# Three of twelve modulation vectors: rows of weights added up on VectorE, one burst of products with ones

## The chip, the cores and the metric

The kernel runs on one core of a Trainium2 chip. The metric is the device time of one execution in microseconds (us). Engines are named as in the profile: PE is TensorE, DVE is VectorE, ACT is ScalarE, POOL is GpSimd, SP is SyncE, which issues nearly all transfers here. Each engine takes its instructions in one fixed order and waits at an instruction until what it needs is there.

## The reference, cut to what matters

Two layers of a diffusion backbone over 384 tokens (128 of a prompt, 256 of a sample). Each layer begins with six modulation vectors of 1024 numbers for each of two conditions:

```
mod = silu(cond) @ w_mod[l] + b_mod[l]          # (1024) @ (1024, 6144)
sh1, sc1, g1, sh2, sc2, g2 = split(mod, 6)      # vectors v = 0 .. 5
h = rms_norm(x, norm1) * (1 + sc1) + sh1
x = x + g1 * token_mixers(h)                    # attention, latent attention, Hyena convolution
h = rms_norm(x, norm2) * (1 + sc2) + sh2
x = x + g2 * conv_ffn(h)
```

So a layer needs vectors 0 and 1 at its first norm, vector 2 at the output projection, 3 and 4 at the second norm, and 5 at the end of the feed-forward part. Twelve vectors in all, written (layer, v) below: (0,0) to (1,5).

## The kernel before

All tokens stand side by side as 384 columns; a product with a 128x128 block of weights is three matmuls of 384 columns (`mm3`, L269 to L271), since weights and activations are split into a high and a low part. A weight load (`load_w`, L249) brings 1 MB into one of two buffers of `raw_ring`; ACT copies the high part (L231), DVE subtracts the low one (L235).

A modulation vector is made by `mod_vec`: four loads of 1 MB (L329, into `raw_ring`, or ahead of time into free slabs by the class `Ahead`), and for each load a burst of four matmuls with 32 weight columns and 512 moving columns (L343), which lie in four column groups of PE and so run side by side. Here the condition is the stationary operand and the weights of the model are the moving one. ACT then copies the sums out of PSUM, PE turns them by four transposes (L302) and DVE adds the bias (L238).

The work is written as Python generators that yield after each step. `weave` advances a main line and, at a rate (steps per step of the main line), side lines: `md` for the modulation vectors, `fl` for the filters of the Hyena part, `att` for attention. The framework's scheduler then puts the instructions of each engine in one order, by the order in which they were written, their priorities, and when it expects operands to be ready. Layer 0 makes vectors 2 to 5 beside its mixers; vectors (1,0) to (1,3) are loaded ahead and made around the norms, where PE has little else; (1,4) follows in layer 1's mixers, (1,5) at its second norm.

A norm (`norm_h`) is a chain over PE, ACT and DVE: sums of squares, square root, `ident` scaled (L391), a product (L394) that spreads the result over partitions; then for each of eight blocks a product on DVE, the modulation on ACT (L402), and a split into high (L409 on DVE, or L231 on ACT) and low (L238 or L235 on DVE) parts `h`. All products of the next stage wait for these blocks.

Names in the rows: `base` holds what lives long (`cT`, the condition; `mods`; `raw_ring`), `split` the split weights, `h` the split activations, `s` the slabs for everything short-lived, `extra` a slab of 3584 columns that attention uses too, `banks` PSUM.

## Time and profile before

| | before |
|---|---|
| median of 3 runs | 1494.21 us (1493.5 to 1496.85) |
| profiled execution | 1491.25 us, span 1489.4 us |
| PE busy | 1443.1 us, 97% of the span |
| DVE busy | 1004.1 us, 67% |
| ACT busy | 752.4 us, 51% |
| matmuls of `mod_vec` | twelve vectors of 4 bursts, 4 matmuls each |

The time of the profiled execution is 1.85 us more than its span, and 2.96 us less than the median. Matmuls are pipelined: the busy time of one overlaps the next, so the cost of a matmul in a stream is the distance from its start to the next start.

### The profile page before, as it was taken

The page shows a single profiled execution, that of the slowest core. Times are in us where ns is not written, and L with a number is a line of the kernel's source. Part 1 is how long each engine was busy: PE and PEld are TensorE (multiplying, and loading weights), DVE is VectorE, ACT ScalarE, POOL GpSimd, SP SyncE. Part 2 cuts the span into 40 slices and gives each one's busy share as a digit, 9 for nine tenths or more (in the row PEclk, how much of TensorE's full clock was granted, in tenths as well). Part 3 has the DMA queues.
Part 4 walks back from the last instruction along what each step waited for, and adds up shares of the span by engine and source line. Part 5 has one row for each costly group of instructions (what it writes and reads, how often), then busy time and mean ns, then how long its engine had stood idle before and what let it go on. Part 6 is the DMA issues. An engine that isn't in the chain of part 4 may idle for free.

```text
span 1489.4 us, 22058 instructions
## 1 busy us (share of the span) xinstructions
PE 1443.1 (97%) x8542; PEld 1334.6 (90%) x8542; DVE 1004.1 (67%) x1920; ACT 752.4 (51%) x1376; POOL 106.1 (7%) x133
## 2 busy tenths in 40 slices
PE   5799999999999999999998999999999999999997
PEld 2598899989888899999996988999998989999997
DVE  6868578547456886686766667874655677566674
ACT  4644366555544663453545444855555465344443
POOL 1223210000000001010000213000000000000000
PEclk9899999999999999999999999999999999999999
DMA  9444454343476533343276445233342534333431
GB/s 364 153 153 141 150 180 142 92 114 114 142 262 223 184 114 113 114 131 114 92 247 207 134 137 185 90 108 98 86 141 87 197 100 134 120 114 123 146 123 48
DMA packets 177497, 212.84 MB, mean 143 GB/s; under 512 B 24177, under 2 KB 160113, under 8 KB 177393
## 3 DMA queue, kind: packets, MB, share of 16 engines
q1 hardware_dynamic: 176528, 206.99, 42.9%
q0 software_dynamic: 864, 4.46, 0.9%
q8 instruction: 67, 1.10, 0.3%
q14 instruction: 38, 0.30, 0.1%
HBM read 209.29 MB, written 2.13 MB: 142 GB/s over the span
## 4 chain that ended last, share of the span: by engine, by line
PE 91%; DVE 5%; ACT 2%; DMA 1%; issue 1%; SPq 0%; DVEq 0%; ACTq 0%
PE banks L269 26%; PE banks L270 26%; PE banks L271 26%; PE banks L302 4%; PE banks L928 3%; PE banks L343 2%; DVE s L238 2%; PE banks L960 2%; DVE split L235 1%; DMA base<-in_w_in_dram 1%; PE banks L564 1%; DVE s L241 1%; ACT split L231 0%; PE banks L509 0%; ACT s L231 0%
## 5 line engine op out<-in xcount | busy, mean ns | idle before, releaser
L231 ACT ACTIVATE split<-base 128x1024 fp32r<-128x1024 f32 (+2 forms) x272 | 280.8, 1040 | 357.4 <-PE banks L270 245.4
L235 DVE TENSOR_TENSOR split<-base,split 128x1024 fp32r<-128x1024 f32 (+2 forms) x272 | 330.4, 1220 | 169.6 <-ACT split L231 169.2
L269 PE MATMUL banks<-h,split 128*128 128x384 f32 x1280 | 432.9, 342 | 6.6 <-DVE h L409 3.6
L270 PE MATMUL banks<-h,split 128*128 128x384 f32 x1280 | 434.3, 340 | 0.0
L271 PE MATMUL banks<-h,split 128*128 128x384 f32 x1280 | 432.6, 338 | 0.5 <-DVE split L235 0.5
L269 PEld LDWEIGHTS banks<-h,split 128*128 128x128 f32 x1280 | 240.9, 189 | 19.0 <-issue 7.9
L270 PEld LDWEIGHTS banks<-h,split 128*128 128x128 f32 x1280 | 241.4, 189 | 4.0 <-DVE h L409 0.8
L271 PEld LDWEIGHTS banks<-h,split 128*128 128x128 f32 x1280 | 241.1, 188 | 2.8 <-DVE split L235 0.8
L271 PE MATMUL banks<-s,split 128*128 128x384 f32 x672 | 225.4, 338 | 0.0
L270 PE MATMUL banks<-s,split 128*128 128x384 f32 x672 | 225.2, 337 | 0.0
L269 PE MATMUL banks<-s,split 128*128 128x384 f32 x672 | 223.5, 339 | 0.8 <-ACT s L231 0.5
L241 DVE SCALAR_TENSOR_TENSOR s<-banks,base,s 128x127 f32<-128x127 f32 (+1 forms) x448 | 172.3, 410 | 11.0 <-ACT s L423 7.1
L231 ACT ACTIVATE s<-banks 128x384 f32<-128x384 f32 (+11 forms) x212 | 94.5, 471 | 94.7 <-PE banks L302 39.6
L231 ACT ACTIVATE s<-s 128x512 fp32r<-128x512 f32 (+3 forms) x142 | 78.9, 561 | 106.3 <-DVE s L238 56.2
L269 PEld LDWEIGHTS banks<-s,split 128*128 128x128 f32 x672 | 125.7, 188 | 4.0 <-ACT s L231 1.0
L271 PEld LDWEIGHTS banks<-s,split 128*128 128x128 f32 x672 | 126.1, 188 | 1.7 <-DVE base L241 0.8
L270 PEld LDWEIGHTS banks<-s,split 128*128 128x128 f32 x672 | 126.1, 188 | 1.3 <-issue 0.2
L238 DVE TENSOR_TENSOR s<-banks,s 128x512 f32<-128x512 f32 (+3 forms) x132 | 81.7, 644 | 37.0 <-PE banks L271 19.4
L241 DVE SCALAR_TENSOR_TENSOR base<-banks,base 128x128 f32<-128x128 f32 (+1 forms) x128 | 46.9, 412 | 73.3 <-PE banks L271 73.3
L238 DVE TENSOR_TENSOR s<-s 128x256 f32<-128x256 f32 (+4 forms) x122 | 68.8, 576 | 27.4 <-ACT s L1231 8.8
L423 ACT ACTIVATE s<-banks,base 128x384 f32<-128x384 f32 x112 | 73.4, 655 | 14.8 <-PE banks L271 14.8
L302 PE MATMUL banks<-base,s 128*128 128x128 f32 x442 | 75.0, 274 | 1.0 <-DVE s L241 0.4
(146 smaller groups left out, 1719.9 us busy)
## 6 DMA issues: line engine op xcount, KB each, us to landing
base<-in_w_in_dram SPq DMA_DIRECT2D x40, 1024.0 KB, 5.5
base<-in_ffn_up_dram SPq DMA_DIRECT2D x40, 1024.0 KB, 5.2
base<-in_w_mod_dram SPq DMA_DIRECT2D x28, 1024.0 KB, 5.4
s<-in_w_mod_dram SPq DMA_DIRECT2D x14, 1024.0 KB, 7.8
base<-in_ffn_down_dram SPq DMA_DIRECT2D x16, 896.0 KB, 4.6
base<-in_w_branch_dram SPq DMA_DIRECT2D x24, 512.0 KB, 3.6
base<-in_w_out_dram SPq DMA_DIRECT2D x8, 1024.0 KB, 5.5
base<-in_ffn_down_dram SPq DMA_DIRECT2D x8, 1024.0 KB, 5.0
```

The source lines that it names most:

```text
L231: act.activation(out=out, in_=in_, func=AF.Copy, scale=scale)
L235: dve.tensor_tensor(out=lo, in0=src, in1=f(hi), op=ALU.subtract)
L238: dve.tensor_tensor(out=out, in0=a, in1=b, op=op)
L241: dve.scalar_tensor_tensor(out=out, in0=a, scalar=s, in1=b, op0=op0, op1=op1)
L269: pe.matmul(out, l[0], r[0], start=start, stop=False)
L270: pe.matmul(out, l[0], r[1], start=False, stop=False)
L271: pe.matmul(out, l[1], r[0], start=False, stop=stop)
L302: pe.transpose(out, in_, ident[:n, :n])
L343: last = pe.matmul(gv[32 * j:32 * j + 32], cT[:, 2 * k + j // 2], raw[:, j // 2, (j % 2) * 512:(j % 2) * 512 + 512], start=k == 0, stop=k ...
L423: act.activation(out=dst, in_=src, func=AF.Identity, scale=vec(l, w1), bias=vec(l, bias))
L928: pe.matmul(out, q_of(h)[:, i * 128:(i + 1) * 128], k, start=m == 0, stop=m == len(ks) - 1)
L960: last = pe.matmul(p[b:b + 64, u], v, pT, start=start, stop=stop, tile_position=(0, b)).ins
```

## The change

The vectors (0,3), (0,5) and (1,4) are made by a new generator `mod_wide`. It loads the weights in 16 pieces of 128 rows by 512 columns (256 KB each) into a ring of three buffers in `extra`. For each piece DVE multiplies the piece by the condition's value for that row and adds it to a sum, once for each of the two conditions (`stt`, 28 instructions of 128x512 for a vector; the first piece of each half is scaled by ACT, 4 instructions). The four sums (two halves, two conditions) are then added over the partitions by four matmuls with 32 columns of ones, in the four column groups. The copy, the four transposes and the bias stay.

The side line of layer 0 is now (0,3), (0,2), (0,4), at rate 0.8 through the Hyena part; (0,5) is woven into the output projection; (1,4) follows the steps woven into layer 0's feed-forward part.

```diff
+R_MW = 0.8
-    XA = Arena([Slab(ctx, tc, N_EXTRA, "extra"), *FA.slabs])
+    extra = Slab(ctx, tc, N_EXTRA, "extra")
+    XO, XA = Arena([extra]), Arena([extra, *FA.slabs])
...
+    def mod_wide(l, v):
+        ring, acc_b = Ring(XO, 3, 512), XO.alloc(2, 2, 512)
+        acc = acc_b.ap()
+        for hf in range(2):
+            col = v * 1024 + hf * 512
+            for k in range(KD):
+                raw = ring.get().ap()
+                sp.dma_start(out=raw, in_=w_mod[l, k * 128:(k + 1) * 128, col:col + 512])
+                for s in range(2):
+                    c, a = cT[:, k, s:s + 1], acc[:, hf, s]
+                    if k:
+                        stt(a, raw, c, a, ALU.mult, ALU.add)
+                    else:
+                        act.activation(out=a, in_=raw, func=AF.Copy, scale=c)
+                yield
+        ring.free()
+        for _ in range(2):
+            yield
+        gv = ps_of("md", 512)
+        last = None
+        for j in range(4):
+            with ExitStack() as order:
+                if last is not None:
+                    order.enter_context(tc.high_priority(offset=U_AV))
+                    order.enter_context(tc.issue_after(last))
+                last = pe.matmul(
+                    gv[32 * j:32 * j + 32], ones[:, 0:32], acc[:, j // 2, j % 2], start=True, stop=True,
+                    tile_position=(0, 32 * j),
+                ).ins
+        acc_b.free()
...
-        md = chain(*[mod_vec(l, v) for v in (2, 3, 4, 5)]) if l == 0 else chain(nxt.pop().steps, mod_vec(l, 4))
+        md = chain(mod_wide(l, 3), mod_vec(l, 2), mod_vec(l, 4)) if l == 0 else nxt.pop().steps
         banks(**PS_HY0)
-        weave(main, (md, R_MD), (fl, R_FL))
+        weave(main, (md, R_MW if l == 0 else R_MD), (fl, R_FL))
...
         finish(md)
+        md = mod_wide(l, 5) if l == 0 else iter(())
...
-        weave(out_proj(l, merged), (ah.loads, R_AH))
+        weave(out_proj(l, merged), (md, R_MW), (ah.loads, R_AH))
+        finish(md)
...
-            weave(main, (fl, R_FL2), (rest, R_RE))
+            weave(main, (fl, R_FL2), (chain(rest, mod_wide(l + 1, 4)), R_RE))
```

Where the instructions come to stand decides much, so three places are shown. Behind the change line numbers are larger by 2 (L238 becomes L240, L241 becomes L243, L269 to L271 become L271 to L273, L302 becomes L304, L343 becomes L345) or by 51 (L388 becomes L439, L409 becomes L460, L564 becomes L615).

First place, the first norm of layer 0. DVE before, from the scale of the norm (the 128x16 instruction of L241) to the first split blocks of `h`:

```order
L241 SCALAR_TENSOR_TENSOR base_101<-base_101 128x16
L238 TENSOR_TENSOR s_1_212<-s_1_147 128x256
L547 RECIPROCAL s_1_147<-s_1_147 128x4
L238 TENSOR_TENSOR s_1_212<-s_1_141 128x256
L409 CAST h_363<-s_1_107 128x384
L238 TENSOR_TENSOR s_1_107<-base_101,banks 128x384
L238 TENSOR_TENSOR h_363<-s_1_107,h_363 128x384
L238 TENSOR_TENSOR s_1_107<-base_101,banks 128x384
```

DVE behind the change, the end of the same stretch (`extra` is the new sum):

```order
L243 SCALAR_TENSOR_TENSOR extra_470<-extra_470,base_101 128x512
L598 RECIPROCAL s_1_147<-s_1_147 128x4
L460 CAST h_363<-s_1_107 128x384
L240 TENSOR_TENSOR s_1_107<-base_101,banks 128x384
L243 SCALAR_TENSOR_TENSOR extra_470<-extra_470,base_101 128x512
L240 TENSOR_TENSOR s_1_107<-base_101,banks 128x384
L460 CAST h_363<-s_1_107 128x384
L240 TENSOR_TENSOR s_1_107<-base_101,banks 128x384 x2
L237 TENSOR_TENSOR h_363<-s_1_107,h_363 128x384 x2
L243 SCALAR_TENSOR_TENSOR extra_470<-extra_470,base_101 128x512
L240 TENSOR_TENSOR h_363<-s_1_107,h_363 128x384
```

The first low part of `h` (the last row) stood two instructions behind the first CAST and stands ten behind it now; nine of the 28 new instructions for (0,3) lie ahead of it, all 28 between the last filter work ahead of the norm and the first outputs of the Hyena products. PE behind the change, where the products with ones of (0,3) come:

```order
L273 MATMUL banks<-h_363,split_362 128x384
L397 MATMUL banks<-extra_470,base_101 32x512 x2
L615 MATMUL banks<-s_1_141 128x256
L615 MATMUL banks<-s_1_212,s_1_141 128x256
L615 MATMUL banks<-s_1_141 128x256
L615 MATMUL banks<-s_1_212,s_1_141 128x256
L304 MATMUL banks<-base_101,s_1_107 128x128
L397 MATMUL banks<-extra_470,base_101 32x512
L603 MATMUL banks<-s_1_141,base_101 128x512
L304 MATMUL banks<-base_101,s_1_107 128x128
L397 MATMUL banks<-extra_470,base_101 32x512
L304 MATMUL banks<-base_101,s_1_107 128x128
```

The four matmuls are no one burst: they stand as two, one and one, with filter products and transposes between. Those of (0,5) stand as two and two, those of (1,4) together.

Second place, the end of layer 0's latent attention on DVE. Before, from the scaling of one softmax (L906) to the split of the outputs (L235 on `banks`):

```order
L904 RECIPROCAL s_5_3170<-s_5_3170 128x1
L906 TENSOR_SCALAR s_5_3170<-s_5_3170 128x384
L235 TENSOR_TENSOR split_362<-base_101,split_362 128x1024
L904 RECIPROCAL s_1_138<-s_1_138 128x1
L906 TENSOR_SCALAR s_1_138<-s_1_138,s_5_3170 128x384
L235 TENSOR_TENSOR split_362<-base_101,split_362 128x1024
L235 TENSOR_TENSOR s_1_135<-banks,s_2_2238 128x2x256
```

Behind the change, from the last softmax's maximum (L948) to the same split:

```order
L948 TENSOR_REDUCE s_5_3192<-banks 128x1
L243 SCALAR_TENSOR_TENSOR extra_470<-extra_470,base_101 128x512
L949 TENSOR_SCALAR s_5_3192<-s_5_3192 128x1
L240 TENSOR_TENSOR base_101<-banks,base_101 128x8 x2
L243 SCALAR_TENSOR_TENSOR extra_470<-extra_470,base_101 128x512 x2
L955 RECIPROCAL s_5_3192<-s_5_3192 128x1
L243 SCALAR_TENSOR_TENSOR extra_470<-extra_470,base_101 128x512
L957 TENSOR_SCALAR s_1_138<-s_1_138,s_5_3192 128x384
L243 SCALAR_TENSOR_TENSOR extra_470<-extra_470,base_101 128x512 x6
L237 TENSOR_TENSOR s_1_135<-banks,s_2_2265 128x2x256
```

The scheduler has pulled (0,5) and the beginning of (1,4) far ahead of where they are written: 38 of the new instructions lie in the last softmaxes of layer 0, four of them inside the last one's chain. The other 18 of (1,4) follow within the last branch and the output projection.

Third place, PE at the second norm of layer 0. Before (L269 is the feed-forward part's first product, L466 a filter product):

```order
L343 MATMUL banks<-s_1_111,base_101 32x512 x4
L343 MATMUL banks<-s_3_3224,base_101 32x512 x4
L343 MATMUL banks<-s_3_3558,base_101 32x512 x4
L343 MATMUL banks<-s_1_138,base_101 32x512 x4
L388 MATMUL banks<-base_101,s_5_3170 128x1 x3
L302 MATMUL banks<-base_101 128x128 x4
L466 MATMUL banks<-s_2_3622 64x384
L394 MATMUL banks<-s_2_3622,base_101 128x384
L343 MATMUL banks<-s_2_3622,base_101 32x512 x4
L343 MATMUL banks<-s_3_2566,base_101 32x512 x4
L343 MATMUL banks<-base_101 32x512 x8
L269 MATMUL banks<-h_363,split_362 128x384 x4
```

Behind the change:

```order
L304 MATMUL banks<-base_101 128x128 x4
L345 MATMUL banks<-s_2_3651,base_101 32x512 x4
L345 MATMUL banks<-s_3_2597,base_101 32x512 x4
L345 MATMUL banks<-base_101 32x512 x4
L439 MATMUL banks<-base_101,s_5_3192 128x1 x3
L517 MATMUL banks<-s_2_3651 64x384
L345 MATMUL banks<-base_101 32x512 x4
L445 MATMUL banks<-s_2_3651,base_101 128x384
L304 MATMUL banks<-base_101 128x128 x4
L271 MATMUL banks<-h_363,split_362 128x384 x4
L397 MATMUL banks<-extra_470,base_101 32x512 x4
L272 MATMUL banks<-h_363,split_362 128x384
```

The four bursts of (1,0) have moved some hundred rows up, into the output projection; behind L445 no burst is left ahead of the first L271, and the products of (1,4) with ones stand right behind it.

## Rows read from the trace of the kernel before

**Rows 1.** The page: busy time of PE and DVE in the span.

```profile
PE 1443.1 (97%) x8542; PEld 1334.6 (90%) x8542; DVE 1004.1 (67%) x1920; ACT 752.4 (51%) x1376; POOL 106.1 (7%) x133
```

**Rows 2.** Windows of 10 us at the first norm; the first line names the columns.

```profile
core 0: us, PE busy (x) PEld busy (x) DVE busy (x) ACT busy (x) POOL busy (x), PEclk, DMA share, GB/s
50.00:60.00 10.00, 4.11 (x20) 2.65 (x20) 10.00 (x17) 2.78 (x4) 3.38 (x2) 0.79 0.35 105
60.00:70.00 10.00, 9.62 (x36) 7.31 (x37) 7.60 (x20) 9.97 (x25) 1.45 (x2) 0.70 0.42 124
```

**Rows 3.** Matmuls of L343 from 50 to 1200 us, in `raw_ring` (two records each).

```profile
L343 PE MATMUL banks<-base x208: 592/592/617, 66.6 to 904.2; 128*32 128x512 f32 x104
```

**Rows 4.** Timeline of PE around a burst alone in a stream.

```profile
253.07 0.34 PE L271 MATMUL banks<-s,split 128*128 128x384 f32 x1
...
253.34 1.07 PE L343 MATMUL banks<-base 128*32 128x512 f32 x8
254.34 0.45 PE L269 MATMUL banks<-s,split 128*128 128x384 f32 x1
254.62 0.34 PE L270 MATMUL banks<-s,split 128*128 128x384 f32 x1
254.79 0.35 PE L271 MATMUL banks<-s,split 128*128 128x384 f32 x1
```

**Rows 5.** Timeline of PE at four bursts in a row.

```profile
1190.77 3.64 PE L343 MATMUL banks<-s,base 128*32 128x512 f32 x32
1194.34 0.83 PE L388 MATMUL banks<-base,s 128*128 128x1 f32 x6
```

**Rows 6.** Timeline of DVE: three multiply-and-add instructions of 128x384.

```profile
448.56 1.49 DVE L241 SCALAR_TENSOR_TENSOR s<-s,s 128x384 fp32r<-128x384 f32 x3
```

**Rows 7.** Timeline of DVE at the first norm of layer 0.

```profile
48.55 1.23 DVE L235 TENSOR_TENSOR split<-base,split 128x1024 fp32r<-128x1024 f32 x1
...
51.41 1.88 DVE L238 TENSOR_TENSOR s<-banks,s 128x512 f32<-128x512 f32 x3
...
60.25 0.16 DVE L241 SCALAR_TENSOR_TENSOR base<-base 128x16 f32<-128x16 f32 x1
...
62.25 0.57 DVE L409 CAST h<-s 128x384 fp32r<-128x384 f32 x1 [0.45 <-ACT s L402]
...
63.21 0.54 DVE L238 TENSOR_TENSOR h<-s,h 128x384 fp32r<-128x384 f32 x1
```

**Rows 8.** Timeline of PE at the first norm and the first Hyena products.

```profile
53.44 1.02 PE L544 MATMUL banks<-base,s 128*128 128x1 f32 x8
60.38 1.22 PE L564 MATMUL banks<-s 128*128 128x256 f32 x2 [5.92 <-DVE s L546]
...
64.92 0.52 PE L270 MATMUL banks<-h,split 128*128 128x384 f32 x1
...
82.89 0.30 PE L302 MATMUL banks<-base,s 128*128 128x128 f32 x1
```

**Rows 9.** Window of the last softmaxes of layer 0; columns as in rows 2.

```profile
387.00:430.00 43.00, 43.00 (x273) 36.05 (x271) 19.52 (x49) 22.28 (x53) 0.00 (x0) 1.00 0.49 163
```

**Rows 10.** Timeline of DVE at the end of layer 0's latent attention.

```profile
425.46 1.23 DVE L235 TENSOR_TENSOR split<-base,split 128x1024 fp32r<-128x1024 f32 x1 [5.88 <-ACT split L231]
```

**Rows 11.** Timeline of PE at the second norm of layer 0.

```profile
479.68 0.83 PE L388 MATMUL banks<-base,s 128*128 128x1 f32 x6
...
482.80 1.92 PE L343 MATMUL banks<-s,base 128*32 128x512 f32 x16
484.54 1.90 PE L343 MATMUL banks<-base 128*32 128x512 f32 x16
486.37 0.97 PE L269 MATMUL banks<-h,split 128*128 128x384 f32 x4
```

**Rows 12.** The page's transfers by size: KB each, median us to landing.

```profile
base<-in_w_mod_dram SPq DMA_DIRECT2D x28, 1024.0 KB, 5.4
...
base<-in_w_branch_dram SPq DMA_DIRECT2D x24, 512.0 KB, 3.6
```

More of the change, by code (lines that the diff above doesn't have):

```diff
@@ L361, in mod_vec @@
         tt(out, out, sums_of[:, 1], ALU.add)
+        if v in (1, 4):
+            o = (V_N1, V_N2)[v // 4]
+            g = vecs[l][:, o:o + 8].unsqueeze(2).to_broadcast([128, 8, 2])
+            stt(avs[l][:, v // 4], mods[l][:, v * 8:v * 8 + 8], 1.0, g, ALU.add, ALU.mult)
+        yield
[16 more added lines that the diff above has]
+        for _ in range(2):
+            yield
+        gv = ps_of("md", 512)
[10 more added lines that the diff above has]
+        acc_b.free()
+        yield
+        copy_a(mod_s.ap(), gv)
+        yield
+        pm = ps_of("md", 4, 128)
+        for q in range(4):
+            transpose(pm[:, q], mod_s.ap()[:, q * 128:(q + 1) * 128])
+        sums_of = pm.rearrange("p q (j s r) -> p j q s r", j=2, s=2)[:, :, :, :, 0]
+        out = mods[l][:, v * 8:v * 8 + 8].rearrange("p (j q) s -> p j q s", q=4)
+        bias = vecs[l][:, V_B + v * 8:V_B + v * 8 + 8].rearrange("p (j q) -> p j q", q=4)
+        for j in range(2):
+            tt(out[:, j], sums_of[:, j], bias[:, j].unsqueeze(2).to_broadcast([128, 4, 2]), ALU.add)
         if v in (1, 4):
@@ L1413 @@
         ch = urgent(chain(hyena_chain(y, 0), hyena_chain(y, 1)), U_CH)
-        weave(hyena_in(y, 1, hT), (md, R_MD), (ch, R_CH))
+        weave(hyena_in(y, 1, hT), (md, R_MW if l == 0 else R_MD), (ch, R_CH))
         while y.late:
```

## Prediction

> **What bounds the kernel now.** First the page: PE is busy in 97% of the span, DVE in 67% [rows 1]. So a removed matmul is a gain, and work on DVE costs nothing as long as no matmul waits for it. Whether one does is read from the stage where the work lands, so the windows come next. At the first norm DVE is full, 10.00 of 10 us, and PE stands at 4.11; in that window and the next PE's granted clock averages 0.79 and 0.70, that is, part of the time at 1.2 instead of 2.4 GHz [rows 2]. It is there that the 28 new DVE instructions of (0,3) have come to stand.
>
> **What a burst costs.** One group of L343 holds 104 matmuls, 26 bursts [rows 3]; the sixteen of layer 0's vectors 2 to 5 and the four of (1,4) are among them, each alone between other products. Around one, PE starts the product ahead of it at 253.07 and the second one behind it at 254.62; two steps of that stream take 2 x 0.17 (254.62 to 254.79), so the burst cost 1.55 - 0.34 = 1.2 us [rows 4]. Four in a row take 1190.77 to 1194.34, 0.89 each [rows 5]. Lone bursts pay 0.3 us more at their edges.
>
> The Trainium skill, TensorEngine Tiling (Array Packing), Key Properties, says that a change of the tiling mode drains TensorE and that different tiles work in parallel. The two prices agree with the first half. It speaks against this change, where three sums come in pieces: by it a piece of one or two matmuls costs what four cost, and the pieces of (0,3) and (0,5) would take 5 x 1.2 = 6.0 us where two whole bursts would take 2.4.
>
> No row shows a split burst. Bounds: a piece of one matmul at no less than its share of a burst in a row, 0.89 / 4 = 0.22, and no more than a lone burst, 1.2. A single matmul of these has the same 592 ns for each of its two records as each of the four that run together [rows 3], so a piece is nearest to a whole burst: I take 1.2.
>
> **Removed and added on PE.** Twelve lone bursts go: 12 x 1.2 = 14.4 us. Pieces come: three for (0,3), two for (0,5), one for (1,4), 6 x 1.2 = 7.2. Copies, transposes and bias stay. So 7.2 us less work on PE if nobody waits; that is the gain that the waits below have to be held against.
>
> **One new DVE instruction.** The trace has no 128x512 of this form. Three multiply-and-adds of 128x384 take 1.49 in all, so 0.47 from start to start [rows 6]; three two-operand instructions of 128x512 take 1.88, 0.60 each [rows 7]. A third more elements on 0.47 gives 0.62 at most, a fixed part less. I take 0.60: 28 are 16.8 us for a vector. ACT's four instructions of a vector lie beside it and cost nothing as long as ACT has its idle time.
>
> **(0,3), at the first norm.** I went down DVE's new order with the durations of the old rows. Both orders agree up to 48.55 [rows 7]. From there the old one reaches the first low part of `h` at 63.75. The new one has nine new instructions ahead of that, 9 x 0.60 = 5.4, and pulls some work of later blocks ahead of it: three products of the norm (0.47 each), two subtractions and a CAST, 2.6. It fills waits of 0.9 us (0.45 for ACT is one) and spares a subtraction that POOL's work had drawn out by 0.9. So 63.75 + 5.4 + 2.6 - 1.8 = 70. PE's first product with a low part started at 64.92 [rows 8] and would start 5 us later; ahead of it PE now has its filter products, done by 64, and little else. Behind that point 19 new instructions (11.4) and 10.9 us of old work (subtractions, six short convolution steps, filters) lie ahead of the end of the last sum: 70 + 22.3 = 92.3. PE reaches its place at some 84 to 87, by how long the clock stays low, and waits at the first transposes and at both single pieces of the burst. The last piece ends at 93.4. The old PE had done as much other work shortly behind 82.89 [rows 8]: with four products of 128x256 (0.22 each), one of 128x512 (0.56) and a transpose (0.2) at 84.5. So PE is 8.9 us late there. In this comparison the old order already holds one burst of (0,2), 1.2, that is still to come now; the four old bursts of (0,3) fall away later, -4.8. Net **+5.3 us**. Bounds: -1.2 if PE finds all in time (three pieces for four bursts); +8.3 if the low clock takes as much again as before (a mean of 0.70 over 10 us is 6 us at half speed, 3 us lost, behind one stop of 5.92 us [rows 2, 8]).
>
> **(0,5), at the end of layer 0's attention.** In the last 43 us of attention DVE was busy for 19.5 us [rows 9]; 38 new instructions add 22.8 and make it 42.3. So DVE goes from half full to full just where each softmax is a chain from PE over DVE and ACT back to PE, and the old slack behind the last softmax, 5.88 us [rows 10], is gone. For the last four score products I followed the chain: PE waits some 1.0 at the second piece of (0,5), 1.6 at the last transposes (3.9 us of DVE work, 2.4 of it new, against 2.2 of PE work to cover it), and 0.5 for ACT's copy. Four bursts go, two pieces come: -4.8 + 2.4 + 3.2 = **+0.8**. Bounds: -2.4 with no wait, +4 with twice the waits.
>
> Loads belong to this: SP's queue is in order, and the new pieces stand among loads of branch weights that wait for `raw_ring`. With three buffers a piece must land about 3 us after its issue; 1 MB takes 5.4 and 0.5 MB 3.6 [rows 12], so 256 KB should take 2.7, an estimate from those. That is just enough, and I put waits for it at 0 here, and in the upper bound.
>
> **(1,4), at the second norm and in layer 1.** Its DVE work ends in the output projection, where DVE waits for PE between steps; that hides it. The four bursts in layer 1 go, -4.8, and the products with ones stand where PE waits for the first low part of `h` anyway, 0. But the old norm was covered by PE's own bursts: from L388 at 479.68 to the first product of the next stage at 486.37, 3.6 us of that bursts behind L394 [rows 11]. The four bursts of (1,0) have moved up, and between L445 and the first L271 nothing is left; PE waits for `h` there some 2.2 us. Net **-2.6**. Bounds: -4.8 with no wait, -1 if the wait takes the whole 3.6.
>
> **Sum**: 5.3 + 0.8 - 2.6 = +3.5 us. On the profiled execution, 1491.25, that is 1494.7; the median of the runs stands 2.96 higher, so 1494.21 + 3.5 = 1497.7.
>
> **The rivals.** A change of 0.2%, 3 us, is about the least that a measurement of this kernel tells from none.
>
> *The gain comes through (faster).* The scheduler expected the sums to be ready at the places where it put the products, and filled with other products where not. If DVE reaches them in time, all three terms fall to their lower bounds, -1.2 - 2.4 - 4.8 = -8.4, and even with the second norm's 2.2 us it is -6: 1487 to 1488. For it: through the last softmaxes PE was busy for 43.00 of 43 us [rows 9], so the old order had its chains well covered. Against it: DVE's 10.00 of 10 us at the first norm [rows 2]. It decides at the first norm: if the first low part of `h` comes under 2 us later, the change is faster.
>
> *Waits half as long (no change).* If the new DVE instructions run into gaps that I count as filled, half of 8.9 + 3.2 + 2.2 falls away, and the sum is -3.6; with two thirds of the waits it is -1.3: 1491 to 1497.
>
> *Loads late (slower still).* If pieces land later than 3 us after issue, behind 1 MB loads, DVE stands at a new instruction with a softmax or a convolution queued behind it. A microsecond for every second piece of (0,3) and (0,5) is 16 us of DVE waits; a third of that on the path gives +9: 1503.
>
> **How the numbers follow.** My sum (+3 to +6) 0.42, half waits 0.30, the gain 0.22, late loads 0.06. The range reaches from the gain's 1487 to 1504. Slower by over 0.2% takes late loads and most of the sum's case; faster takes the gain and a little of the half waits: faster 0.25, no change 0.31, slower 0.44.
>
> **What would show it.** Right: in the changed trace the new instruction takes 0.60 us; the first product with a low part of `h` starts near 70, not 65; PE waits for DVE ahead of the single pieces near 85 to 92; it waits 1 to 2 us at the last transposes of layer 0's attention and 2 us behind L445; 865 to 905 us of layer 1 loses four bursts. Wrong: PE's windows from 60 to 100 as full as before, or a piece of one matmul in far less than 1.2 us, or waits of DVE for `extra`'s loads, which I have at zero.

## The result, and the profile after

The changed kernel takes 1520.18 us (median of 4 runs, 1517.99 to 1522.41) against 1493.89 for the kernel before (4 runs): a ratio of 1.0167, 95% interval 1.0151 to 1.0184. By that ratio it is 25 us slower (26 by the two medians), where 1497.7 was predicted and 1504 was the upper end of the range. Every difference in us below is worked out in the same way, from the ratio and some 1494 us. The profiled execution took 1522.41 us, its span 1520.6.

The page's busy times, the row that answers to [rows 1]:

```profile
PE 1451.9 (95%) x8470; PEld 1341.8 (88%) x8470; DVE 1059.6 (70%) x2004; ACT 760.6 (50%) x1388; POOL 111.0 (7%) x133
```

PE has 72 records fewer and is busy longer. So the span has to be read by stretches. I cut both at the same four places of the program: behind the first norm and filters of layer 0, at the last products of its attention, at the first products of its feed-forward, and at the end. Windows of the kernel before (columns as in [rows 2]):

```profile
0.00:105.00 105.00, 80.43 (x408) 58.03 (x409) 71.09 (x141) 53.87 (x103) 21.70 (x32) 0.95 0.63 219
105.00:426.25 321.25, 318.72 (x1941) 284.20 (x1939) 204.18 (x389) 171.03 (x347) 27.18 (x38) 1.00 0.45 140
426.25:500.00 73.75, 73.72 (x460) 65.01 (x457) 50.84 (x104) 36.76 (x61) 1.28 (x2) 1.00 0.73 252
500.00:1489.40 989.40, 970.27 (x5741) 927.33 (x5739) 677.95 (x1289) 490.71 (x867) 55.90 (x61) 0.99 0.40 127
```

The same stretches of the changed kernel:

```profile
0.00:115.00 115.00, 84.62 (x384) 57.22 (x385) 91.12 (x167) 56.28 (x105) 21.98 (x31) 0.91 0.63 216
115.00:447.85 332.85, 321.78 (x1922) 289.19 (x1920) 225.33 (x425) 175.60 (x355) 30.30 (x39) 0.98 0.45 139
447.85:535.50 87.65, 79.82 (x456) 67.42 (x457) 69.67 (x132) 38.75 (x64) 1.10 (x2) 0.92 0.66 225
535.50:1520.60 985.10, 965.72 (x5713) 927.93 (x5711) 673.45 (x1282) 489.96 (x865) 57.66 (x61) 1.00 0.39 124
```

The three stretches that hold the new DVE work grew by 10.0, 11.6 and 13.9 us; the last one, which lost four bursts, shrank by 4.3. DVE's busy time grew by 19 to 21 us in each of the three, about one vector in each: 28, 32 and 24 of the 84 new instructions start there. PE's busy time grew too, because part of it now runs at the low clock (0.91, 0.98 and 0.92 on average). The reader should split each stretch in three: **idle** (length less busy), **lost clock** (busy time times one less the granted clock, added up over windows of 5 us), and the rest, PE's **work** at full clock. For the whole span, before to after: idle 46.2 to 68.7, +22.4; lost clock 4.3 to 18.2, +13.8; work 1438.8 to 1433.8, -5.1; together +31.2. The difference of the medians is smaller, because the profiled execution of before is 3 us below its median and that of the changed kernel 2 us above. Work fell, as it was meant to. What PE waits for, and the low clock behind the waits, took it back seven times over.

**First stretch.** Windows answering to [rows 2], and beyond them:

```profile
60.00:70.00 10.00, 4.58 (x11) 2.97 (x11) 10.00 (x17) 7.42 (x18) 2.34 (x2) 0.66 0.66 194
70.00:80.00 10.00, 8.46 (x29) 7.00 (x30) 10.00 (x21) 6.26 (x13) 0.00 (x0) 0.66 0.44 129
...
90.00:100.00 10.00, 7.44 (x26) 3.10 (x24) 10.00 (x21) 3.49 (x7) 0.29 (x1) 1.00 0.46 132
```

DVE is full in all three, PE stands, and its clock averages 0.66 in the first two, 60 to 80 us; in [rows 2] the low clock lay in 50 to 70, and was over by 70, as the next window of the kernel before shows:

```profile
70.00:80.00 10.00, 10.00 (x57) 9.69 (x56) 3.69 (x8) 5.37 (x11) 0.00 (x0) 1.00 0.25 87
```

PE's timeline in the changed kernel there (start, duration, then the idle time before it and what ended it):

```profile
63.25 1.22 PE L615 MATMUL banks<-s 128*128 128x256 f32 x2 [6.92 <-DVE s L597]
...
68.66 0.80 PE L271 MATMUL banks<-h,split 128*128 128x384 f32 x3 [1.62 <-DVE h L460]
71.53 2.05 PE L603 MATMUL banks<-s,base 128*128 128x512 f32 x2 [2.08 <-DVE s L240]
73.51 0.69 PE L272 MATMUL banks<-h,split 128*128 128x384 f32 x1
...
90.92 1.05 PE L397 MATMUL banks<-extra,base 128*32 128x512 f32 x4
92.99 0.70 PE L615 MATMUL banks<-s 128*128 128x256 f32 x2 [1.01 <-DVE s L597]
...
96.35 1.05 PE L397 MATMUL banks<-extra,base 128*32 128x512 f32 x2 [0.66 <-DVE extra L243]
...
99.11 1.05 PE L397 MATMUL banks<-extra,base 128*32 128x512 f32 x2
```

The stop of 5.92 us [rows 8] is now 6.92, and two more stops follow it. The first product with a low part starts at 73.51 instead of 64.92, at the low clock. L397 is the split burst: a piece of one matmul (two records) takes 1.05 us, as much as one of two.

**Second and third stretch.** DVE's timeline at the end of attention, at the split of the attention outputs and at the first residuals:

```profile
432.43 1.41 DVE L243 SCALAR_TENSOR_TENSOR extra<-extra,base 128x512 f32<-128x512 f32 x2 [2.72 <-DMA extra<-in_w_mod_dram]
...
434.23 0.41 DVE L957 TENSOR_SCALAR s<-s 128x384 f32<-128x384 f32 x1
...
449.74 4.06 DVE L243 SCALAR_TENSOR_TENSOR extra<-extra,base 128x512 f32<-128x512 f32 x6 [3.07 <-DMA extra<-in_w_mod_dram]
453.72 1.01 DVE L237 TENSOR_TENSOR s<-banks,s 128x512 fp32r<-128x512 f32 x2
...
478.91 4.07 DVE L243 SCALAR_TENSOR_TENSOR extra<-extra,base 128x512 f32<-128x512 f32 x6 [1.66 <-DMA extra<-in_w_mod_dram]
482.89 1.39 DVE L243 SCALAR_TENSOR_TENSOR base<-banks,base 128x128 f32<-128x128 f32 x4
```

And PE, from the last softmaxes to the second norm:

```profile
434.79 0.52 PE L304 MATMUL banks<-base,s 128*128 128x128 f32 x3 [2.47 <-DVE s L957]
437.31 1.65 PE L979 MATMUL banks<-s,s 128*128 128x384 f32 x2 [2.00 <-ACT s L951]
445.28 0.44 PE L271 MATMUL banks<-s,split 128*128 128x384 f32 x1 [1.37 <-ACT s L233]
...
447.85 0.44 PE L1011 MATMUL banks<-s,s 128*64 128x256 f32 x2 [0.58 <-ACT s L233]
...
454.78 0.44 PE L272 MATMUL banks<-s,split 128*128 128x384 f32 x1 [2.16 <-DVE s L237]
...
508.28 1.92 PE L345 MATMUL banks<-s,base 128*32 128x512 f32 x16 [1.88 <-DVE base L240]
...
514.71 1.65 PE L445 MATMUL banks<-s,base 128*128 128x384 f32 x2
...
519.21 1.65 PE L271 MATMUL banks<-h,split 128*128 128x384 f32 x4 [2.00 <-DVE h L460]
520.78 1.93 PE L397 MATMUL banks<-extra,base 128*32 128x512 f32 x8
```

Two engines read together: the six new instructions at 449.74 stand ahead of L237, for which PE waits at 454.78. They wait 3.07 us themselves for a piece that has not landed, and take 4.06. In the same way DVE stands 2.72 us for a piece of (0,5) until 432.43, ahead of the scaling (L957) for which PE waits 2.47 us at 434.79. The second norm's products and the burst of (1,4) then run at half clock (1.65 us, where [rows 11] has 0.97 for the same four, and 1.93).

That the instructions crowd there is not the scheduler's choice alone. The pieces lie in `extra`, which attention uses too. Attention's products read it until 399.88 us; SP stands until then and issues the second piece of (0,5) at 399.90; the first multiply-and-add of (0,5) starts at 404.2. In the runs with (0,5) or (1,4) alone (below) it is the same: `extra` is read until 389.62 and 389.37, and the second piece is issued at 389.65 and 389.39.

### The profile page after: what moved, and what is told of

Its sections match the earlier page's. It is cut to its first block, busy times and chain, and to the rows that moved or that the text cites. A ratio compares the mean times of both kernels' runs of the same rounds, so it can differ in the third digit from the quotient of the medians.

```text
span 1520.6 us, 22097 instructions
## 1 busy us (share of the span) xinstructions
PE 1451.9 (95%) x8470; PEld 1341.8 (88%) x8470; DVE 1059.6 (70%) x2004; ACT 760.6 (50%) x1388; POOL 111.0 (7%) x133
## 4 chain that ended last, share of the span: by engine, by line
PE 80%; DVE 8%; DMA 6%; ACT 3%; issue 2%; SPq 0%; POOL 0%; DVEq 0%; ACTq 0%
PE banks L271 24%; PE banks L273 23%; PE banks L272 23%; PE banks L304 3%; DVE s L240 3%; PE banks L979 2%; DMA base<-in_w_in_dram 2%; DVE extra L243 2%; DVE split L237 2%; DMA extra<-in_w_mod_dram 2%; PE banks L1011 1%; PE banks L345 1%; DVE s L243 1%; DMA base<-in_w_mod_dram 1%; DMA s<-in_p_w_dram 1%
## 5 line engine op out<-in xcount | busy, mean ns | idle before, releaser
L271 PE MATMUL banks<-h,split 128*128 128x384 f32 x1280 | 432.3, 341 | 10.9 <-DVE h L460 7.2
L273 PE MATMUL banks<-h,split 128*128 128x384 f32 x1280 | 433.1, 339 | 0.7 <-DVE split L237 0.7
L237 DVE TENSOR_TENSOR split<-base,split 128x1024 fp32r<-128x1024 f32 (+2 forms) x272 | 328.5, 1211 | 143.7 <-ACT split L233 143.1
L271 PEld LDWEIGHTS banks<-h,split 128*128 128x128 f32 x1280 | 241.8, 189 | 17.9 <-DVE h L460 9.9
L273 PEld LDWEIGHTS banks<-h,split 128*128 128x128 f32 x1280 | 241.8, 189 | 3.1 <-DVE split L237 1.0
L271 PE MATMUL banks<-s,split 128*128 128x384 f32 x672 | 224.5, 341 | 2.7 <-ACT s L233 2.5
L273 PE MATMUL banks<-s,split 128*128 128x384 f32 x672 | 226.6, 340 | 0.0
L243 DVE SCALAR_TENSOR_TENSOR s<-banks,base,s 128x127 f32<-128x127 f32 (+1 forms) x448 | 172.4, 410 | 7.6 <-ACT s L474 3.7
L233 ACT ACTIVATE s<-banks 128x384 f32<-128x384 f32 (+10 forms) x212 | 94.6, 473 | 129.9 <-PE banks L304 56.9
L271 PEld LDWEIGHTS banks<-s,split 128*128 128x128 f32 x672 | 125.9, 188 | 5.8 <-ACT s L233 3.2
L273 PEld LDWEIGHTS banks<-s,split 128*128 128x128 f32 x672 | 126.7, 189 | 2.7 <-DVE base L243 0.8
L240 DVE TENSOR_TENSOR s<-banks,s 128x512 f32<-128x512 f32 (+3 forms) x132 | 81.8, 644 | 35.4 <-PE banks L273 18.3
L243 DVE SCALAR_TENSOR_TENSOR base<-banks,base 128x128 f32<-128x128 f32 (+1 forms) x128 | 46.8, 412 | 67.2 <-PE banks L273 67.1
L240 DVE TENSOR_TENSOR s<-s 128x256 f32<-128x256 f32 (+4 forms) x122 | 69.4, 580 | 28.3 <-ACT s L1282 9.7
L304 PE MATMUL banks<-base,s 128*128 128x128 f32 x442 | 76.1, 275 | 4.7 <-DVE s L957 2.5
L237 DVE TENSOR_TENSOR s<-s,s 128x384 fp32r<-128x384 f32 (+2 forms) x102 | 66.7, 657 | 19.8 <-ACT s L233 13.1
```

The source lines that it names most:

```text
L233: act.activation(out=out, in_=in_, func=AF.Copy, scale=scale)
L237: dve.tensor_tensor(out=lo, in0=src, in1=f(hi), op=ALU.subtract)
L240: dve.tensor_tensor(out=out, in0=a, in1=b, op=op)
L243: dve.scalar_tensor_tensor(out=out, in0=a, scalar=s, in1=b, op0=op0, op1=op1)
L271: pe.matmul(out, l[0], r[0], start=start, stop=False)
L273: pe.matmul(out, l[1], r[0], start=False, stop=stop)
```

## The experiments

The theory at the start: the loss is DVE's own new work, which the scheduler puts ahead of work that PE waits for. The rival: late loads in SP's queue. Times are medians, with the ratio to the kernel before on the same chip. The table at the end of this section has idle and lost clock of the kernels that the argument rests on.

**One vector at a time.** The other two stay bursts. The edit for (0,3) is shown; it keeps the rate 0.8, while with (0,5) or (1,4) alone layer 0's modulation goes at 0.24, as before the change:

```diff
-md = chain(mod_wide(l, 3), mod_vec(l, 2), mod_vec(l, 4)) if l == 0 else nxt.pop().steps
+md = chain(mod_wide(l, 3), *[mod_vec(l, v) for v in (2, 4, 5)]) if l == 0 else chain(nxt.pop().steps, mod_vec(l, 4))
...
-        md = mod_wide(l, 5) if l == 0 else iter(())
+        md = iter(())
...
-            weave(main, (fl, R_FL2), (chain(rest, mod_wide(l + 1, 4)), R_RE))
+            weave(main, (fl, R_FL2), (rest, R_RE))
```

> Of the three vectors only (0,3) goes the new way; (0,5) and (1,4) are bursts as before. Theory (DVE's queue is in order, and the new instructions stand ahead of the first norm's and the filters' work): the whole lateness that the changed kernel shows by the end of layer 0's gates, +15.2 us, comes from this vector alone: 1509 us, and the first product with a low part of h again near 73. Rival (the three lines of pieces together overload SP's queue, no single one is dear): a third of the loss, about +9: 1503.

1506.83 us, 1.0083 (1.0065 to 1.0101): +12.4 us. The first product with a low part starts at 73.72, and DVE stood only 0.4 us for a piece in the whole run.

> Of the three vectors only (0,5) goes the new way. Theory (DVE full through the last softmaxes, and standing at pieces that come late behind branch weights): the lateness gained between the gates' end and the split of the attention outputs in the changed kernel, 23.9 - 15.2, about +8.7: 1503 us. Rival (the loss there was caught from (0,3), a clock that had not recovered): the +0.8 of the prediction: 1495.

1501.1 us, 1.0041 (1.0027 to 1.0054): +6.1.

> Of the three vectors only (1,4) goes the new way. Theory: what the changed kernel loses from the split of the attention outputs to the second norm, 31.3 - 23.9 = 7.4 us, belongs to this vector's first pieces, and four bursts in layer 1 go, -4.8: about +2.6: 1497 us. Rival (that loss belongs to the last pieces of (0,5), and this vector is hidden): -2.6 as predicted: 1491.

1499.47 us, 1.0026 (1.0016 to 1.0037): +3.9. The three add up to 22.4 of the 25, so each loses by itself. But the third is not the term that was looked for. With (0,5) out of the way, (1,4)'s instructions are hoisted further up, into the last softmaxes (394.9 to 429.2 us, where those of (0,5) lie in its own run):

```profile
L243 DVE SCALAR_TENSOR_TENSOR extra<-extra,base x28: 727/744/753, 394.9 to 429.2; 128x512 f32<-128x512 f32 x28
```

**Loads without products, products without loads.** In the first, DVE does only the second block of each half; in the second, only one piece of each half is loaded:

```diff
-                    if k:
+                    if k == 1:
                         stt(a, raw, c, a, ALU.mult, ALU.add)
-                    else:
+                    elif k == 0:
```

```diff
-                raw = ring.get().ap()
-                sp.dma_start(out=raw, in_=w_mod[l, k * 128:(k + 1) * 128, col:col + 512])
+                if k == 0:
+                    raw = ring.get().ap()
+                    sp.dma_start(out=raw, in_=w_mod[l, k * 128:(k + 1) * 128, col:col + 512])
```

> All three vectors go the new way and all 48 pieces are loaded, but 12 of the 84 new DVE instructions are left (only those of the second block of rows of each half; the sums are of two blocks in place of eight). DVE's waits for most pieces go with them. Theory (the loss is DVE's own new work and what stands behind it): no more than before, 1487 to 1495 us. Rival (the pieces in SP's queue hold up the weight loads behind them, whatever DVE does): at least half of the 26 us stays, 1507 or more.

1493.31 us, 0.9985 (0.9974 to 0.9997): -2.2.

> All three vectors go the new way with all 84 new DVE instructions, but only the first of the eight pieces of each half is loaded and all products read it (so the sums are of one block eight times): six loads in place of 48, and DVE waits for hardly any. Theory (the loss is DVE's own new work ahead of the norms, softmaxes and splits): at least two thirds of the 26 us stay, 1511 us or more. Rival (DVE and the weight loads wait for late pieces in SP's queue): most of it goes, 1502 or less.

1528.06 us, 1.0223 (1.0208 to 1.0238): +33.3, worse than with the loads. DVE waits for no piece, and its instructions go in earlier and denser (55 of the 84 start in attention, not 32), and PE's idle time before the end of attention is 52 us against 41.5 with the loads (table). Both point the same way, and so does (0,3) alone: the loss does not need late pieces, it needs the products. That the late pieces cost nothing is not shown. DVE stood 8.1 us for four of them in the changed kernel (below), two of these times right ahead of a stop of PE, and in neither run here do the products stand where they stand there.

**The price of the new instruction.**

```diff
-                        stt(a, raw, c, a, ALU.mult, ALU.add)
+                        stt(a, raw, 0.5, a, ALU.mult, ALU.add)
```

> As the changed kernel, but each new DVE instruction multiplies by the number 0.5 in place of a column of the conditioning vector (so the sums are weighed wrongly). Theory (it is the column that makes the instruction dearer than the prediction's 0.60): 0.68 us in place of 0.745, start to start 0.60; 84 times 0.06 is 5 us less on DVE, some 3 of it on the path: 1517 us. Rival (the price goes by the size alone): 0.745 stays and the time is the changed kernel's 1520.

1522.56 us, 1.0175 (1.0157 to 1.0194): the changed kernel's time. The price did fall, as all instructions on `extra` show (minimum, median, maximum in ns), first of the changed kernel, then of this one:

```profile
L243 DVE SCALAR_TENSOR_TENSOR extra<-extra,base x84: 729/745/2333, 50.0 to 494.9; 128x512 f32<-128x512 f32 x84
its engine sat idle before it (us, times) until:
  DMA extra<-in_w_mod_dram: 8.1, 4
```

```profile
L243 DVE SCALAR_TENSOR_TENSOR extra<-extra x84: 655/684/2072, 51.7 to 488.5; 128x512 f32<-128x512 f32 x84
```

So the column costs 60 ns, 5 us in all, and no part of it is seen in the time. The theory was right on the price and wrong on its weight.

**Held to the written place.** A load is put behind the last weight load written before it, a new DVE instruction behind the last two-operand instruction written before it:

```diff
+                with tc.issue_after(at_sp[0]):
                     sp.dma_start(out=raw, in_=w_mod[l, k * 128:(k + 1) * 128, col:col + 512])
...
+                        with tc.issue_after(at_dve[0]):
                             stt(a, raw, c, a, ALU.mult, ALU.add)
```

> As the changed kernel, with the same work, but each piece's load is held behind the last weight load that the program has written before it on SP, and each new DVE instruction behind the last two-operand instruction written before it on DVE: so nothing of (0,3) stands ahead of the first norm, and (1,4) lies in the feed-forward. Theory (the place costs, not the amount): PE has twelve bursts less and three to six pieces more, -8 to -11, and some waits in the output projection, where (0,5) now lies, +0 to +5: 1483 to 1491 us. Rival (55 us more on DVE and 48 loads more cost wherever they lie): at least half the loss stays, 1507 or more.

1530.09 us, 1.0233 (1.022 to 1.0247): the expectation failed, and the time is in the rival's range. The first stretch is as before the change (idle 26.0, lost clock 3.4). But (0,5), written into the output projection, now ends among the second norm's instructions, and PE stands 5.76 us for DVE's first split block there. The window of this kernel at the second norm:

```profile
490.00:500.00 10.00, 2.43 (x7) 1.70 (x7) 10.00 (x20) 5.13 (x12) 0.00 (x0) 0.50 0.28 79
```

DVE full, PE a quarter busy, at the low clock throughout. It is the same cause at another place, where I had put it myself. Whether the work costs wherever it lies, as the rival has it, the next run answers.

> Only (1,4) goes the new way, held to its written place as above: its 28 instructions lie spread over the feed-forward of layer 0 in place of the last softmaxes of layer 0's attention, where the run with (1,4) alone had them. Theory: four bursts go and one comes, DVE's 21 us hide: -3.6, 1491 us. Rival (the loads or the DVE work cost there too): 1494 to 1499, as with (1,4) alone.

1495.17 us, 1.0002 (0.9992 to 1.0011): no loss, but no gain either. No new instruction waits there, and the stretches up to the feed-forward are as before within 2 us (table). So the DVE work and the loads cost nothing there, against the rival, although the time is in its range. The gain is missing because the burst comes in three pieces:

```profile
664.75 1.05 PE L401 MATMUL banks<-extra,base 128*32 128x512 f32 x4
...
674.65 1.04 PE L401 MATMUL banks<-extra,base 128*32 128x512 f32 x2
...
677.07 1.05 PE L401 MATMUL banks<-extra,base 128*32 128x512 f32 x2
```

Three pieces of 1.05 us for four bursts of 0.95 (the run with one burst of four, below) leave a gain of 0.65 us.

> Only (0,3) goes the new way, and its loads and DVE instructions are held to their written place, which is behind the first norm (the first of them behind the 80th instruction of DVE's queue). Theory (its 12.4 us came from standing ahead of the norm and the filters): all of it goes, and of the four bursts saved for three pieces something between 0 and -3.7 is left: 1490.5 to 1494.5 us. Rival (19 us of DVE work cost wherever they lie in the first 200 us): at least half stays, 1500 us or more.

1505.18 us, 1.0065 (1.0052 to 1.0078): +9.7, where nothing was expected; the rival's number came true. The first stretch did heal, from 32.4 us idle and 5.2 lost clock with (0,3) hoisted to 26.3 and 3.4. The second got worse: PE's stops between 300 and 330 us, which the kernel before does not have, apart from a stop of 1.71 us ahead of 314.15, which it has too:

```profile
301.84 0.94 PE L306 MATMUL banks<-base,s 128*128 128x128 f32 x6 [0.19 <-DVE s L239]
303.42 0.55 PE L306 MATMUL banks<-base,s 128*128 128x128 f32 x3 [0.65 <-ACT extra L235]
...
328.79 0.64 PE L273 MATMUL banks<-h,split 128*128 128x384 f32 x1 [2.32 <-ACT split L235]
```

**The gain by itself.** In the kernel before, the three vectors do one burst of four:

```diff
+            few = (l, v) in ((0, 3), (0, 5), (1, 4))
-            for j in range(4):
+            for j in range(0 if few and k else 4):
```

> The kernel before, with all loads, but (0,3), (0,5) and (1,4) do one burst of four in place of four (so these three vectors are sums over a quarter of the rows): nine lone bursts fewer and nothing new on DVE. This is the gain side by itself. Theory of the prediction (a lone burst is 1.2 us on the path, wherever it stands): -10.8, 1483.5 us. Rival (many of the bursts had filled stops of PE, and without them it waits): about a third of that, 1490 to 1492.

1487.27 us, 0.9947 (0.9934 to 0.9961): -7.9 for nine bursts, 0.9 each. In the profile work falls by 8.6 us, 0.95 a burst. That is nearer to the prediction's price than to the rival's third: the bursts were on the path.

**The rate.** The changed kernel also steps layer 0's modulation at 0.8 per main step instead of 0.24. First that alone in the kernel before, then (0,3) alone with the bursts behind it slowed again:

```diff
-        weave(main, (md, R_MD), (fl, R_FL))
+        weave(main, (md, 0.8 if l == 0 else R_MD), (fl, R_FL))
...
-        weave(hyena_in(y, 1, hT), (md, R_MD), (ch, R_CH))
+        weave(hyena_in(y, 1, hT), (md, 0.8 if l == 0 else R_MD), (ch, R_CH))
```

```diff
+    def slow(g):
+        for _ in g:
+            yield
+            yield
+            yield
...
-chain(mod_wide(l, 3), *[mod_vec(l, v) for v in (2, 4, 5)])
+chain(mod_wide(l, 3), slow(chain(*[mod_vec(l, v) for v in (2, 4, 5)])))
```

> The kernel before, with one number changed: in the two weaves of layer 0's Hyena part the modulation steps are taken at 0.8 per main step, the changed kernel's R_MW, in place of 0.24. No vector goes the new way. Theory (a term that the prediction did not have: at this rate the bursts of layer 0 come earlier and the attention's chains lose what had filled PE's stops): +5 us or more, 1499 or above. Rival (the rate moves bursts and nothing else): 1492 to 1497 us.

1497.19 us, 1.0015 (1.0006 to 1.0024): +2.2, a small term at most, measured in the old order of the vectors.

> (0,3) alone the new way and held to its written place, and the bursts of (0,2), (0,4), (0,5) behind it at 0.27 per main step in place of 0.8. Theory (of the +9.8 of the run with (0,3) held, which no longer lost at the first norm, the rest is the rate's): 1491 to 1496 us. Rival (it is the new DVE work in the 200 us behind the norm): 1502 us or more.

> (0,3) alone the new way, where the scheduler puts it (ahead of the first norm), and the bursts behind it at 0.27 in place of 0.8. Theory of the rate: of the +12.4 at the fast rate some 8 go, 1498 to 1500 us, the 5 left being the first norm's. Rival (the loss at the first norm carries through): 1505 us or more.

1530.3 us, 1.023 (1.0212 to 1.0248), and 1528.72 us, 1.0231 (1.0217 to 1.0245). Neither total answers the question. The steps came so late that the last eight bursts lie between 421 and 467 us, up to the middle of the output projection, where PE stands 10 us for a load of 1 MB. PE in the first of the two:

```profile
447.76 1.92 PE L347 MATMUL banks<-base 128*32 128x512 f32 x16 [1.31 <-DVE base L242]
459.76 1.94 PE L347 MATMUL banks<-base 128*32 128x512 f32 x8 [10.08 <-DMA base<-in_w_mod_dram]
```

Up to the end of attention the two can be read: idle and lost clock there are 5.8 and 1.5 us, and 3.7 and 0.0, some 3 us less each than at the rate 0.8 (7.3 and 3.1, 4.8 and 1.6 in the table). So the rate may have had a part in attention's loss; the difference is little more than what the table is good for, and bursts are missing from that stretch.

**The third stretch.** The changed kernel, with (1,4) alone held:

```diff
-                with tc.issue_after(at_sp[0]):
+                with tc.issue_after(at_sp[0]) if l else ExitStack():
...
-                        with tc.issue_after(at_dve[0]):
+                        with tc.issue_after(at_dve[0]) if l else ExitStack():
```

> The changed kernel, all three vectors the new way, with (0,3) and (0,5) where the scheduler puts them and (1,4) alone held to its written place in the feed-forward. In the changed kernel (1,4) stands ahead of the splits of the output projection and of the second norm, and the stretch from the last attention product to the first products of the feed-forward took 13.9 us longer than before. Theory (that stretch is (1,4)'s DVE work): it falls back to some 74 us, and the whole to 1506 to 1510 us. Rival (the stretch is late pieces and a low clock that (0,5) leaves behind): 10 us or more of it stay, 1515 us or above.

1512.21 us, 1.0115 (1.0097 to 1.0132): +17.2 instead of +25. Its window from the last attention products to the feed-forward:

```profile
442.03:515.90 73.87, 73.19 (x453) 64.63 (x453) 50.12 (x101) 36.30 (x60) 1.10 (x2) 1.00 0.66 225
```

87.65 us are 73.87 again, with DVE at 50.12 instead of 69.67 busy and PE never at the low clock. The stretch was (1,4)'s instructions there, with DVE's waits for their pieces (3.07 and 1.66 us); the run moves both and does not part them. The whole fell by 8 us, less than the stretch and 2 short of the theory's range; in part because (1,4) then takes three pieces in the feed-forward, as above, instead of one (PE's work is 2.5 us more).

Idle and lost clock of PE in the four stretches, and its work in the whole span, in us, worked out from the windows as explained in the first section (a row is good to some 2 us):

```
kernel                    first norm  attention  proj., 2nd norm  rest      work
before                    24.6 / 2.9   2.5 / 0.0    0.0 / 0.0   19.1 / 1.5  1438.8
changed                   30.4 / 7.3  11.1 / 3.9    7.8 / 5.5   19.4 / 1.5  1433.8
(0,3) alone               32.4 / 5.2   4.8 / 1.6    0.8 / 0.0   20.0 / 1.3  1439.6
(0,3) alone, held         26.3 / 3.4   7.3 / 3.1    1.0 / 0.0   20.0 / 4.2  1439.4
(1,4) alone, held         24.9 / 4.6   2.6 / 0.0    0.0 / 0.0   20.6 / 2.5  1438.6
(0,5) alone               23.9 / 4.3   8.1 / 3.8    0.6 / 0.0   18.9 / 2.8  1437.7
(1,4) alone               24.1 / 4.7   6.6 / 1.6    0.7 / 0.0   19.9 / 4.4  1438.4
changed, few products     22.8 / 2.6   6.2 / 0.0    0.7 / 0.0   20.3 / 2.6  1434.4
changed, few loads        34.8 /11.1  17.2 / 2.6    0.7 / 0.8   19.5 / 2.9  1434.6
changed, all held         26.0 / 3.4   8.2 / 0.0   11.8 / 4.5   27.8 / 5.4  1439.1
changed, (1,4) held       30.5 / 4.9   9.1 / 3.1    0.7 / 0.0   21.0 / 2.6  1436.3
before, one burst of four 25.0 / 3.5   2.6 / 1.4    0.7 / 0.0   20.5 / 1.2  1430.3
```

## Why the prediction was wrong

**The sum of the three terms failed in each of them.** The direction had the largest chance of the three, but the size was outside the range, and for one reason: waits were counted where I had followed a chain, put at nothing elsewhere, and the low clock behind them was left out of the sum. The three terms hold 11.9 us of waits (6.5, 3.2 and 2.2); PE's idle time grew by 22.4 us, and 13.8 us of lost clock came on top. The 6.5 is the 8.9 us of lateness less the pieces, 3.6, plus the burst of (0,2), 1.2; the rival with half the waits halves the whole 8.9, which is a slip: half the waits give -2.5, not -3.6.

*Bursts and pieces.* Right in kind. A lone burst was taken at 1.2 us; nine that are left out give 0.9 each. A piece of one matmul was taken as dear as a burst; it takes 1.05, a burst 1.06. The Trainium skill, TensorEngine Tiling (Array Packing), Key Properties, states that different tiles work in parallel and that a change of the tiling mode drains TensorE. The trace agrees with the first: four side by side take as long as one; what the drain costs by itself no run here shows. Twelve bursts at 0.95 less six pieces at 1.05 are 5.1 us, what the profile shows (5.1) and less than the 7.2 of the prediction. That the two agree so closely is in part luck: 0.95 is a difference of work, 1.05 a duration.

*The new instruction.* Predicted 0.60 us; it takes 0.745, and 0.67 from start to start (six take 4.07 in all). I had read multiply-and-adds with immediates [rows 6]; the one with a column is 60 ns dearer. The immediates bought no time back, so this is not why the sum was off.

*(0,3): +5.3 predicted (to +8.3), +12.4 measured alone.* The mechanism was right: the first low part of `h` late, PE waiting ahead of the single pieces. The step that failed is the one from "ahead of it PE now has its filter products, done by 64, and little else": the stops and the low clock that follow from it got no price of their own. PE lost 1 us more in the stop before 63.25, 1.62 at 68.66 and 2.08 at 71.53, and the low clock behind these stops lay in 60 to 80 us, where [rows 2] had it in 50 to 70. The first product with a low part came 8.6 us late, not 5, and the last piece ended at 100.16, where by the prediction's own mark the old kernel had done as much at 84.5: 15.7 us late, not 8.9. With (0,3) alone the first stretch holds 7.8 us more of idle time and 2.3 more of lost clock than before. The low clock had been seen as a reason for the upper bound only; it belonged in the sum. Not all of the 12.4 is this place: 3.9 of the 16.1 us between the two profiled spans lie in attention, and the run has the faster rate, to which the prediction gave no term.

*(0,5): +0.8 predicted (to +4), +6.1 alone.* The waits came where they were put, at the last transposes and softmaxes, but there were four (2.47, 2.00, 1.37, 0.58 us) and not three of together 3.2, and the low clock behind them was not in the sum. Ahead of the first of them DVE stands 2.72 us for a piece, a wait that the prediction put at zero. In the changed kernel PE's clock averages 0.79 and 0.87 from 430 to 450.

*The loads at zero.* Wrong as a statement: pieces of 256 KB took 3.1 us (median) to land, not 2.7, and DVE stood for them 8.1 us. But the run with all loads and few products was not slower than before, and products without loads lost more. The rival "loads late" is therefore not needed for the loss; what the waits of 2.72, 3.07 and 1.66 us added to it in the changed kernel no run here parts from the products.

*(1,4): -2.6 predicted.* The step that failed is "DVE waits for PE between steps; that hides it". Twelve of its instructions are not between steps: six stand ahead of the split for which PE waits at 454.78, six ahead of the first residuals at 482.89. The stretch took 13.9 us more, and the run with (1,4) held took those back. The wait that was predicted behind L445, 2.2 us, is there with 2.00. The four bursts in layer 1 are gone, as predicted: the last stretch is 4.3 us shorter.

*What is open.* (0,3) held behind the first norm no longer loses there but loses 9.7 us all the same; in the profiles 7.9 of the 15.2 us between the spans lie in attention. The stops at 300 to 312 us are also in the run with few products, so the amount of new DVE work does not make them; the run with one burst of four does not have them, so missing bursts alone do not either. The rate by itself gave 2.2 us, and its trace does not have these stops. What is left is a guess: another order of the attention's chains against the main stream. The two runs at a slower rate were to show it and ran into another stop. So the cause of that part stays open. No version that does all the work beats the kernel before, and the run that leaves out most of the products gains 2.2 us: even nearly free products would leave the change little.

## What to carry to other kernels

Price a move of work to a half-busy engine by what stands behind each instruction in that engine's queue, at every place where the scheduler puts it, and ask when the buffer that it needs comes free; the share of busy time says nothing on that. The same 19 us of a vector changed the time by 0 us in the feed-forward, by +4 to +6 in the softmaxes, by +12 with the first norm behind it, and by +10 right behind that norm for a reason not found, its saved bursts counted. And where PE's stops come close together, add the low clock behind them: here 13.8 us of lost clock on 22.4 of idle.

## What the hardware showed beside that

A multiply-and-add of 128x512 on DVE takes 745 ns with a column as its scalar and 684 with a number. A piece of one 128*32 matmul takes TensorE 1.05 us, as long as a burst of eight records (1.06); at the low clock such a burst takes 1.93. A load of 256 KB lands in 3.1 us (median of 48), where one of 1024 KB of the same weights takes 5.4 or 6.8 (by where it lands): a quarter of the bytes in about half the time.
